# A list scheduler's durations of TensorE instructions replaced by others: the same 13,025 instructions in another order

## Chip, cores and metric

The kernel runs on one core of one Trainium2 chip. The metric is device time in microseconds (us) of one execution; the number compared is the median of several runs of the same program. Five engines run side by side, each with its own stream of instructions in a fixed order: TensorE (PE for its products, PEld for the loads of its weights), VectorE (DVE), ScalarE (ACT), GpSimd (POOL) and SyncE (SP, which issues the transfers).

## What is computed

Two blocks of two layers each on 256 tokens of 1024 features, in fp32, with a memory of 256 tokens. Cut to what matters:

```python
def first_block(x, mem, ...):
    for l in range(DEPTH):                                   # DEPTH = 2
        x = x + 0.5 * swiglu(rms_norm(x, ffn1_norm[l]), ffn1_w_in[l], ffn1_w_out[l])
        z = rms_norm(x, mix_norm[l]) @ w_mix_in[l]
        z_mla, z_swa, z_na = jnp.split(z, [MLA_IN, MLA_IN + SWA_IN], axis=-1)
        o = jnp.concatenate([rms_norm(mla_mixer(z_mla, ...), ...),   # latent attention, 8 heads
                             rms_norm(swa_mixer(z_swa, ...), ...),   # windowed, 4 heads
                             rms_norm(na_mixer(z_na, ...), ...)])    # neighbourhood, 4 heads
        x = x + o @ w_mix_out[l]
        x = x + mem_xattn(rms_norm(x, mem_norm_x[l]), mem, ...)
        x = x + 0.5 * swiglu(rms_norm(x, ffn2_norm[l]), ffn2_w_in[l], ffn2_w_out[l])
        x = rms_norm(x, block_norm[l])
```

The second block has, per layer, a mixer of two attentions (one of three branches with compressed keys, 8 heads, and one over blocks, "MoBA", 8 heads), gates of the branches, an output product and a third feed-forward, all modulated by columns worked out from a condition vector.

## The kernel before

**Products.** Every weight is an fp32 matrix that arrives in chunks of 128 x 1024 (`wr`, 512 KB). `wload` (line 455) splits a chunk into a high part `wh` (a cast, on ACT or DVE) and a low part `wl` (a subtraction, on DVE). The activations are split the same way into `xh` and `xl` (or two tiles `g`). `mm3` (line 481) then issues three fp32r products for each pair of operands (`wh`,`xh`; `wl`,`xh`; `wh`,`xl`), 128 x 512 at most, and `proj` (line 487) sums them over the k-tiles for both token tiles of 128. The 8570 instructions of TensorE are 6984 such fp32r products, 56 in bf16 (masks), and 1530 in plain fp32: transposes against an identity (`ps<-ident,g`) and the small products of the attentions.

**Between products.** The head norms and rotations of a projection (`heads` at line 1170, the latent part of `mixer` at line 759) are a chain: a product ends in PSUM; ACT squares it; DVE sums it per head; POOL raises the sums to the power -1/2 (`rstd`, line 429); DVE multiplies, rotates in four operations and adds; TensorE transposes the outcome. A softmax (`softmax_rows`, line 550) is a chain of the same kind: scores, DVE maximum, ACT exponential, DVE reciprocal, a scaling on ACT or DVE, four transposes.

**What sets the order.** The program is first traced in its natural order into a `Plan` as 13,025 instructions, each with its dependences. `Plan.schedule` (line 257) plays them through on paper: each engine has a time at which it is free, each instruction a duration from the table `Plan.cost` (line 231), and a result reaches TensorE from another engine `slack` = 400 ns after its end. At each step an engine takes, of the instructions that could start within 25 ns of the earliest (TensorE; other engines use a share of the duration), the one that stands first in the trace. So where TensorE would have to wait for a chain, a product of a later projection goes in between, and the transposes that the chain ends in go in as soon as the plan believes them ready:

```python
first = min(found, key=lambda f: f[:2])                       # line 328
lim = first[0] + (window if e == "tensor" else wait_for * cost(first[2], e))
s, pr, o = min((f for f in found if f[0] <= lim), key=lambda f: f[1])
...
e = min(o.ways, key=lambda w: max(free[w], at) + cost(o, w) + (spare if w == "vector" else 0))
```

The last line chooses ACT or DVE for an instruction that both can do. `emit` (line 385) then hands all instructions to their engines in that order, which is why every row of the profile bears line 385. On the chip nothing is reordered: an engine whose next instruction is not ready waits. The rest of the table, for the engines other than TensorE, is the same before and after the change (n: elements per partition):

```python
if eng == "gpsimd":
    return 300.0 + 165.0 * n if fn == "tensor_tensor" else 150.0
...
if eng == "scalar":
    return (51 if psum else 93) + n / 1.2 + 93 * cols
...
return 69 + n / (1.92 if fast else 0.96) + 62 * col          # DVE
```

Of the kernel before, what the change touches and what calls it, by code (L numbers as in the profile page):

```python
# [10 lines left out]
F32R = mybir.dt.float32r  # L11
BF = mybir.dt.bfloat16
# [6 lines left out]
# buffers: weight chunks (raw, split), transposed operands, activations of 1 and 2 KB a partition,  # L19
# columns, PSUM banks (and how many of them the attention may hold)  # L20
B = {"wr": 7, "wh": 7, "wl": 7, "xh": 4, "xl": 4, "g1": 11, "g2": 36, "sm": 40, "ps": 8, "psa": 6}
TAIL = (10, 12)      # k-tiles of a feed-forward's output halves in which one token tile goes ahead
# places in the trace by which some instructions give way to later ones
HP = (100, 3)        # products of the compression: the first, and each after it
XN = 300             # the block norm of the residual
XS = (43, 52, 60)    # parts of the input
# [10 lines left out]
CH = 1024          # columns of a weight chunk  # L37
# [21 lines left out]
# The kernel is traced in its natural order into a Plan. The Plan gives every  # L59
# instruction its place in the engines' streams by list scheduling (an engine takes  # L60
# the earliest instruction of the trace whose operands and buffers are there), and
# then hands them to Tile in that order. Tile places the buffers and the waits.

TABLE = {AF.Exp: 1, AF.Tanh: 1, AF.Silu: 2, AF.Sin: 3}     # which activations share a table


class VTile:
    def __init__(self, plan, pool, shape, dtype, tag, bufs, psum, share):
# [4 lines left out]
        self.acc = []                    # (op, p0, p1, mask, write, start)  # L73
        self.first = self.last = None    # trace positions
# [3 lines left out]
class View:  # L78
    """A slice of a tile: what it covers, and how to make it from the real one."""
# [81 lines left out]
class Plan:  # L161
# [6 lines left out]
    def tile(self, pool, shape, dtype, tag, bufs=1, psum=False, share=None):  # L168
        """share: (name, n): at most n of the tag's buffers may be held under that name"""
# [7 lines left out]
    @contextmanager  # L177
    def shift(self, by):
        """instructions traced inside rank as if they came `by` places later"""
        self.bias += by  # L180
        yield
        self.bias -= by

    # ---- tracing
    def either(self, *ways):
        """one instruction that several engines can carry out: (engine, fn, args, kw)"""
        return self.record(*ways[0], others=ways[1:])
# [1463 lines left out]
```

## Time and profile before

| | |
|---|---|
| median of 3 runs | 1945.27 us (1941.7 to 1947.16) |
| profiled execution: span from its first to its last instruction | 1940.7 us |
| profiled execution: time outside the span | not recorded |
| TensorE busy (products) | 1905.7 us, 98% of the span |
| DVE, ACT, POOL busy | 1438.1, 874.7, 119.9 us |
| read from HBM | 360.38 MB, 186 GB/s over the span |

How to read it: a product is in flight longer than it holds the engine, and the next one starts before it ends; a "busy" TensorE therefore also hides short gaps, and the distance from one start to the next tells the real pace. An instruction's idle time is put down to the engine whose result came last.

### The profile page before, as it was taken

To read this page: it belongs to the slowest core of one execution; us is meant where nothing else is said; L and a number is where in the kernel's file an instruction comes from. 1 tells how busy PE (TensorE), PEld (TensorE's weight loads), DVE (VectorE), ACT (ScalarE), POOL (GpSimd) and SP (SyncE) were. 2 spreads that over 40 slices of the span, in tenths; PEclk is the share of its full clock that TensorE was granted. 3 is DMA by queue.
4 is the path that set the end of the run, shared out by engine and by line. 5 is a ranking of instruction groups with operands and counts; after the bars stand their busy time and mean duration, and the time that the engine had idled before them with its cause. 6 is when DMAs were issued, how large, how long until landed. Compare 5 with 4: busy or idle time off the path is not lost.

```text
span 1940.7 us, 24909 instructions
## 1 busy us (share of the span) xinstructions
PE 1905.7 (98%) x9061; PEld 1512.4 (78%) x9062; DVE 1438.1 (74%) x2330; ACT 874.7 (45%) x1664; POOL 119.9 (6%) x98
## 2 busy tenths in 40 slices
PE   8999999999999999999999999999999999999999
PEld 6888867788887888767888766787888857787887
DVE  7875887898688866878986667578865867487664
ACT  5331675643243434657442455534431455435431
POOL 0000301100000001301000112000000102000000
PEclk9999999999999999999999999999999999999999
DMA  8776523388578856235885432357855513454561
GB/s 306 266 253 208 180 97 98 117 316 289 185 246 300 276 192 185 75 98 167 295 274 193 143 131 87 125 186 232 297 187 186 184 44 120 141 183 165 191 198 65
DMA packets 105242, 363.05 MB, mean 187 GB/s; under 512 B 13216, under 2 KB 15136, under 8 KB 105120
## 3 DMA queue, kind: packets, MB, share of 16 engines
q1 hardware_dynamic: 105120, 361.47, 55.5%
q8 instruction: 71, 1.16, 0.2%
q14 instruction: 51, 0.42, 0.1%
HBM read 360.38 MB, written 1.05 MB: 186 GB/s over the span
## 4 chain that ended last, share of the span: by engine, by line
PE 85%; DVE 7%; ACT 3%; POOL 3%; DMA 1%; issue 1%; SPq 0%; POOLq 0%; ACTq 0%; DVEq 0%
PE ps L385 85%; POOL sm L385 3%; DVE g L385 2%; ACT g L385 2%; DVE sm L385 2%; DVE wl L385 1%; DMA wr<-ffn_in_in 1%; DVE x L385 1%; DVE wh L385 0%; ACT wh L385 0%; ACT junk L385 0%; DMA inv<-inv_in 0%; DMA wr<-in_qa_in 0%; DMA x<-x_in 0%; ACT xh L385 0%
## 5 line engine op out<-in xcount | busy, mean ns | idle before, releaser
L385 DVE TENSOR_TENSOR wl<-wr,wh 128x1024 fp32r<-128x1024 f32 (+1 forms) x572 | 689.8, 1214 | 76.2 <-ACT wh L385 59.0
L385 PE MATMUL ps<-wh,xh 128*128 128x512 f32 (+3 forms) x1600 | 626.3, 392 | 3.6 <-ACT xh L385 1.3
L385 PE MATMUL ps<-wh,xl 128*128 128x512 f32 (+3 forms) x1600 | 623.4, 390 | 0.2 <-DVE xl L385 0.2
L385 PE MATMUL ps<-wl,xh 128*128 128x512 f32 (+3 forms) x1600 | 620.1, 388 | 0.0
L385 ACT CAST wh<-wr 128x1024 fp32r<-128x1024 f32 (+1 forms) x370 | 386.0, 1045 | 307.4 <-PE ps L385 279.8
L385 PE MATMUL ps<-wh,g 128*128 128x512 f32 (+1 forms) x1456 | 460.8, 393 | 0.2
L385 PEld LDWEIGHTS ps<-wh,xh 128*128 128x128 f32 x1600 | 302.2, 189 | 60.9 <-ACT xh L385 2.6
L385 PEld LDWEIGHTS ps<-wh,xl 128*128 128x128 f32 x1600 | 301.7, 189 | 58.6 <-DVE xl L385 1.8
L385 PEld LDWEIGHTS ps<-wl,xh 128*128 128x128 f32 x1600 | 302.1, 189 | 54.9 <-issue 1.5
L385 PEld LDWEIGHTS ps<-wh,g 128*128 128x128 f32 x1456 | 271.9, 188 | 57.4 <-issue 3.0
L385 PE MATMUL ps<-wl,g 128*128 128x512 f32 (+1 forms) x728 | 285.0, 392 | 0.0
L385 ACT ACTIVATE g<-ps,sm 128x256 f32<-128x256 f32 (+5 forms) x337 | 157.3, 488 | 169.4 <-PE ps L385 155.4
L385 POOL TENSOR_TENSOR sm<-sm,mhalf 128x1 f32<-128x1 f32 (+6 forms) x76 | 117.0, 1541 | 1474.8 <-DVE sm L385 1440.6
L385 DVE CAST wh<-wr 128x1024 fp32r<-128x1024 f32 (+2 forms) x202 | 139.0, 689 | 90.3 <-PE ps L385 89.4
L385 PE MATMUL ps<-ident,g 128*128 128x128 f32 (+1 forms) x942 | 157.3, 276 | 18.6 <-DVE g L385 10.7
L385 PEld LDWEIGHTS ps<-ident,g 128*128 128x128 f32 (+1 forms) x942 | 111.0, 141 | 78.8 <-ACT g L385 22.7
L385 PE MATMUL ps<-g,g 128*64 128x256 f32 (+8 forms) x728 | 171.8, 375 | 0.3
L385 DVE TENSOR_TENSOR g<-ps,g 128x256 f32<-128x256 f32 (+3 forms) x158 | 89.7, 568 | 109.2 <-ACT g L385 71.5
L385 PEld LDWEIGHTS ps<-wl,g 128*128 128x128 f32 x728 | 136.8, 188 | 28.4 <-issue 1.7
L385 PEld LDWEIGHTS ps<-g,g 128*64 128x64 f32 (+5 forms) x728 | 91.8, 161 | 52.1 <-issue 17.8
L385 ACT ACTIVATE junk<-x 128x512 bf16<-128x512 f32 x56 | 35.3, 630 | 189.1 <-DVE x L385 184.4
L385 ACT COPY g<-ps 128x512 f32<-128x512 f32 (+5 forms) x173 | 76.9, 467 | 93.2 <-PE ps L385 89.4
(93 smaller groups left out, 1008.1 us busy)
## 6 DMA issues: line engine op xcount, KB each, us to landing
wr<-ffn_in_in SPq DMA_DIRECT2D x264, 512.0 KB, 4.6
wr<-ffn_out_in SPq DMA_DIRECT2D x132, 512.0 KB, 4.2
wr<-ada_in SPq DMA_DIRECT2D x96, 512.0 KB, 4.7
wr<-in_gate_in SPq DMA_DIRECT2D x32, 512.0 KB, 3.5
wr<-in_b_in SPq DMA_DIRECT2D x24, 512.0 KB, 4.6
wr<-mix_out_in SPq DMA_DIRECT2D x16, 512.0 KB, 4.6
wr<-w_out_in SPq DMA_DIRECT2D x16, 512.0 KB, 4.6
wr<-mix_swa_in SPq DMA_DIRECT2D x8, 512.0 KB, 5.2
```

The lines of the kernel that those rows point to most:

```text
L385: getattr(getattr(self.nc, o.eng), fn)(*[r(a) for a in args], **{k: r(v) for k, v in kw.items()})
```

## The change

Two lines of `Plan.cost` give other durations (ns) for TensorE's products. Nothing else that is executed differs (the file also lost its comments, which have no effect).

```diff
@@ Plan.cost
         if eng == "tensor":
             if fn == "transpose":
                 return 109.0
             if ins[0].dtype == F32:
-                return max(n * 4 / 2.4, 213.0) * (0.52 if outs[0].shape[0] <= 64 else 1.0)
-            return max(n / 2.4, 107.0 if ins[0].dtype == F32R else 53.0) + 2.5
+                return 2 * max(n * 2 / 2.4 + 2, 109.0)
+            return max(n / 2.4 + 14, 109.0 if ins[0].dtype == F32R else 67.0)
```

An fp32r product of 512 columns goes from 215.8 to 227.3 ns, of 256 columns from 109.2 to 120.7; a plain fp32 product of 256 columns from 426.7 to 430.7, or from 221.9 to 430.7 where its output has at most 64 partitions (probabilities times values).

The order changes from the first mixer on; the feed-forwards keep theirs but for a few places. Of the casts and copies that ACT or DVE may do, five casts of weights (`wh<-wr`) go from ACT to DVE (365 and 207 of 572 instead of 370 and 202). Three places follow. `g2_88` and the like are tiles of activations, `ps` PSUM banks, the numbers behind names are those of buffers, and a row with x4 is four transposes.

TensorE, first block, first layer, latent attention: the transposes of the second token tile's normed queries and keys (`g2_88`, `g2_92`) among the products of the neighbourhood projection that fill the time of the chain. Before:

```order
L385 MATMUL ps_2249<-wh_2027,xl_1830 128x512
L385 MATMUL ps_2249<-wh_2027,xh_1822 128x512
L385 MATMUL ps_2249<-wl_2038,xh_1822 128x512
L385 MATMUL ps_2286<-ident_69,g2_88 128x128 x4
L385 MATMUL ps_2292<-ident_69,g2_92 128x128 x4
L385 MATMUL ps_2249<-wh_2067,xh_1822 128x512
```

And now:

```order
L385 MATMUL ps_2253<-wl_2027,xh_1562 128x512
L385 MATMUL ps_2253<-wh_2016,xl_1572 128x512
L385 MATMUL ps_2279<-ident_69,g2_88 128x128 x4
L385 MATMUL ps_2287<-ident_69,g2_92 128x128 x4
L385 MATMUL ps_2253<-wh_2029,xh_1821 128x512
L385 MATMUL ps_2253<-wl_2036,xh_1821 128x512
```

The eight transposes stand five 512-column products earlier, counted from the product that starts their chain.

TensorE, second block, first layer, MoBA: the transposes of the first token tile's keys (`g2_11154` before, `g2_11150` now) among the products of the next projection. Before:

```order
L385 MATMUL ps_11211<-wh_11107,xl_10117 128x512
L385 MATMUL ps_11211<-wh_11169,xh_10102 128x512
L385 MATMUL ps_11252<-ident_69,g2_11154 128x128 x4
L385 MATMUL ps_11211<-wl_11200,xh_10102 128x512
L385 MATMUL ps_11211<-wh_11169,xl_10117 128x512
```

And now:

```order
L385 MATMUL ps_11209<-wh_11063,xh_10092 128x512
L385 MATMUL ps_11209<-wl_11119,xh_10092 128x512
L385 MATMUL ps_11221<-ident_69,g2_11150 128x128 x4
L385 MATMUL ps_11209<-wh_11063,xl_10097 128x512
L385 MATMUL ps_11209<-wh_11074,xh_10092 128x512
```

Between the last product of these keys' own projection and the transposes stood 43 products of 512 columns, and 29 stand there now. For the second tile's keys it was 43 and is 33. The second layer has the same pattern.

DVE at the same place, the norm and rotation of these keys (`TENSOR_REDUCE` is the sum per head, `TENSOR_SCALAR` what POOL waits for, the rows from there on the rotation). Before:

```order
L385 TENSOR_REDUCE sm<-g_11162 128x8
L385 TENSOR_SCALAR sm<-sm 128x8
L385 TENSOR_TENSOR wl<-wr,wh 128x1024 x2
L385 TENSOR_TENSOR g_11154<-g_11154,sm 128x512
L385 TENSOR_TENSOR g_11234<-g_11154,g_9027 128x512
L385 TENSOR_TENSOR g_11239<-g_11154,g_9027 128x8x32 x2
L385 TENSOR_TENSOR g_11154<-g_11234,g_11239 128x512
```

And now:

```order
L385 TENSOR_REDUCE sm<-g_11155 128x8
L385 TENSOR_SCALAR sm<-sm 128x8
L385 TENSOR_TENSOR wl<-wr,wh 128x1024
L385 CAST wh<-wr 128x1024
L385 TENSOR_TENSOR g_11150<-g_11150,sm 128x512
L385 TENSOR_TENSOR g_11196<-g_11150,g_8822 128x512
L385 TENSOR_TENSOR g_11203<-g_11150,g_8822 128x8x32 x2
L385 TENSOR_TENSOR g_11150<-g_11196,g_11203 128x512
```

A cast has taken the place of one of the two subtractions; the chain itself has the same rows.

## Rows read from the trace of the kernel before

**Rows 1.** The page: busy us by engine (share of the span) and count.
```profile
PE 1905.7 (98%) x9061; PEld 1512.4 (78%) x9062; DVE 1438.1 (74%) x2330; ACT 874.7 (45%) x1664; POOL 119.9 (6%) x98
```

**Rows 2.** The page: the chain that ended last, by engine.
```profile
PE 85%; DVE 7%; ACT 3%; POOL 3%; DMA 1%; issue 1%; SPq 0%; POOLq 0%; ACTq 0%; DVEq 0%
```

**Rows 3.** Stretches: length, PE, PEld, DVE, ACT, POOL busy; clock, DMA share, GB/s.
```profile
200.00:300.00 100.00, 94.84 (x511) 73.83 (x510) 81.26 (x184) 70.56 (x179) 20.80 (x13) 1.00 0.40 129
...
1400.00:1500.00 100.00, 100.00 (x451) 82.43 (x450) 65.17 (x73) 29.55 (x40) 0.00 (x0) 1.00 0.60 196
```

**Rows 4.** Timeline of PE, 600 to 606 us: start, length (us), instruction.
```profile
600.57 0.40 PE L385 MATMUL ps<-wh,xh 128*128 128x512 f32 x1
...
605.82 0.39 PE L385 MATMUL ps<-wh,xl 128*128 128x512 f32 x1
```

**Rows 5.** Timeline of PE, 262 to 276 us: probabilities times values, two records each.
```profile
263.12 1.08 PE L385 MATMUL ps<-g,g 128*64 128x256 f32 x4
264.13 0.39 PE L385 MATMUL ps<-wh,xl 128*128 128x256 f32 x1
```

**Rows 6.** Groups by form: count | busy us, mean ns | idle before and releasers.
```profile
L385 DVE TENSOR_TENSOR wl<-wr,wh 128x1024 fp32r<-128x1024 f32 x554 | 672.4, 1222 | 67.6 <-ACT wh L385 50.5
...
L385 ACT CAST wh<-wr 128x1024 fp32r<-128x1024 f32 x357 | 375.0, 1052 | 265.9 <-PE ps L385 245.4 <-DMA wr<-ffn_in_in 9.9 <-DMA wr<-in_kv_in 3.4
...
L385 DVE CAST wh<-wr 128x1024 fp32r<-128x1024 f32 x197 | 136.1, 692 | 88.3 <-PE ps L385 87.4 <-DMA wr<-ffn_in_in 0.7
...
L385 POOL TENSOR_TENSOR sm<-sm,mhalf 128x8 f32<-128x8 f32 x16 | 38.0, 2378 | 167.3 <-DVE sm L385 154.1 <-ACT wh L385 11.5 <-ACT g L385 1.7
```

**Rows 7.** The chain of waits, 222 to 256 us: start, length, what.
```profile
237.14 5.28 POOL sm L385
```

**Rows 8.** Timeline of PE, 242 to 245 us; in brackets idle time and releaser.
```profile
241.80 0.39 PE L385 MATMUL ps<-wl,xh 128*128 128x512 f32 x1
244.07 1.17 PE L385 MATMUL ps<-ident,g 128*128 128x128 f32 x8 [1.88 <-DVE g L385]
```

**Rows 9.** Timeline of PE, second block, first layer: chain's last product, then its transposes.
```profile
1194.63 0.39 PE L385 MATMUL ps<-wh,xl 128*128 128x512 f32 x1
...
1204.88 0.39 PE L385 MATMUL ps<-wh,xh 128*128 128x512 f32 x1
1205.50 0.63 PE L385 MATMUL ps<-ident,g 128*128 128x128 f32 x4 [0.23 <-DVE g L385]
1205.89 0.48 PE L385 MATMUL ps<-wl,xh 128*128 128x512 f32 x1
```

**Rows 10.** Timeline of PE: the same transposes in the second layer.
```profile
1628.64 0.63 PE L385 MATMUL ps<-ident,g 128*128 128x128 f32 x4 [0.25 <-DVE g L385]
```

**Rows 11.** Timeline of DVE, 1198 to 1212 us.
```profile
1202.54 0.69 DVE L385 TENSOR_TENSOR g<-g,sm 128x512 f32<-128x512 f32 x1 [0.39 <-POOL sm L385]
```

**Rows 12.** A stretch of 10 us, second block, first layer (columns as in rows 3).
```profile
1200.00:1210.00 10.00, 9.77 (x46) 7.79 (x45) 9.09 (x13) 5.06 (x10) 4.94 (x2) 1.00 0.47 159
```

**Rows 13.** Timeline of PE: second layers of both blocks, two transposes at the end of chains.
```profile
795.85 0.63 PE L385 MATMUL ps<-ident,g 128*128 128x128 f32 x4 [0.73 <-DVE g L385]
...
1537.61 0.63 PE L385 MATMUL ps<-ident,g 128*128 128x128 f32 x4 [0.69 <-ACT wh L385]
```

**Rows 14.** Timeline of PE: waits in attention whose products are now longer covered.
```profile
362.25 0.50 PE L385 MATMUL ps<-wh,xh 128*128 128x512 f32 x1 [0.46 <-ACT g L385]
...
381.00 0.41 PE L385 MATMUL ps<-ident,g 128*128 128x128 f32 x2 [0.36 <-DVE g L385]
...
808.01 0.77 PE L385 MATMUL ps<-ident,g 128*128 128x128 f32 x5 [1.33 <-ACT g L385]
...
855.06 0.66 PE L385 MATMUL ps<-ident,g 128*128 128x128 f32 x4 [0.48 <-ACT g L385]
```

**Rows 15.** Stretches of 10 us with a lower granted clock (columns as in rows 3).
```profile
1110.00:1120.00 10.00, 10.00 (x62) 9.00 (x61) 8.07 (x11) 5.31 (x8) 0.52 (x1) 0.83 0.69 219
...
1590.00:1600.00 10.00, 10.00 (x32) 4.66 (x33) 3.15 (x11) 4.87 (x18) 0.00 (x0) 0.72 0.00 0
```

## The prediction

> **What bounds the kernel now.** I read the page first: products keep TensorE busy 98% of the span, DVE 74%, ACT 45% [rows 1]. The page's chain agrees: 85% of the way to the end is TensorE's own work, and the rest, some 15%, runs over DVE, ACT and POOL [rows 2]. The stretches of 100 us then show where that rest lies: 100.00 of 100 us busy in a feed-forward (1400 to 1500 us), 94.84 in the first mixer (200 to 300 us), where DVE and ACT are also fullest [rows 3]. The change issues the same instructions, so it can only win or lose the gaps of the mixers, and the order shows that the feed-forwards hardly move.
>
> Busy time hides short gaps, so the pace has to come from starts: from 600.57 to 605.82 us there are 24 products of 512 columns, 23 steps, 0.228 us each [rows 4]. That is the new table's 227.3 ns, not the old 215.8. Probabilities times values, 64 partitions out, take (264.13 - 263.12)/2 = 0.505 us each [rows 5]: the old table said 0.222, the new one says 0.431. So the new figures are nearer the chip. But a plan lives by the ratio of TensorE's time to that of the chains it covers, and the other engines keep figures that are too short: DVE's subtraction of 1024 elements is planned at 1.14 us and takes 1.222, its cast 0.60 against 0.692, ACT's cast 0.95 against 1.052, POOL's power of 8 columns 1.62 against 2.378 [rows 6]. Before, everything was planned too fast by similar shares; now only the chains are.
>
> **The first latent chain.** At 237.14 us POOL begins the power of 16 columns, planned at 300 + 16 x 165 ns = 2.94 us; it takes 5.28, and DVE's rotation follows [rows 7]. TensorE's last product before the transposes starts at 241.80, they start at 244.07: the step is 2.27 instead of 0.228 us, so some 2.0 us are lost, of which 1.88 shows as idle on DVE [rows 8]. There was no spare cover, and the new order takes five products away: 5 x 0.228 = **+1.1 us**, if the chain is no quicker.
>
> **MoBA's keys, twice.** From the keys' last product (1194.63) to their transposes (1205.50) pass 10.9 us, and the transposes already wait: 1204.88 to 1205.50 is 0.62 instead of 0.23 us [rows 9]. Of 43 covering products 29 remain: 14 x 0.228 = 3.2 us. The second tile's keys lose ten products, 2.3 us, but their chain runs while TensorE waits for the first, so I count the larger alone. Could the chain shorten instead? DVE is busy 9.09 of 10 us there [rows 12], and the order keeps its rows. One subtraction gives way to a cast, 1.222 to 0.692 us [rows 6], but both stand between DVE's hand-over to POOL and POOL's answer, where DVE waits 0.39 us for POOL in any case [rows 11]. So nothing is gained. The second layer shows the same wait, at 1628.64 us [rows 10], and the same cuts: 2 x 3.2 = **+6.4 us**. If the second tile's cut came on top, 2 x 2.3 = 4.6 more.
>
> **Second layers.** The transposes at 795.85 us waited 0.73 us [rows 13]. Their cover loses 29 products of 512 columns and 3 of half that length (30.5 x 0.228 = 7.0 us) and gains 8 score products, 6 transposes and 2 masks: 8 x 0.505 [rows 5], 6 x 0.1 (four take 1205.89 - 1205.50 = 0.39 us) [rows 9], 2 x 0.228 = 5.1 us. The scores' and masks' prices are borrowed from the rows that they are nearest to. **+1.9 us**. The transposes at 1537.61 waited 0.69 [rows 13]; they lose one product and some small ones: between 0.2 and 1.4 us, taken **+0.8**.
>
> **What is gained.** Four waits get more cover than they miss: 0.46, 0.36, 1.33 and 0.48 us [rows 14], together **-2.6**. In the first mixer's attention up to eight products that stood ahead of transposes now stand behind them; ACT's stream there is shortened too, by work moved behind, so this is between 0 and 8 x 0.228 = 1.8 us a layer, taken as 0 because TensorE was ready late there, not early. The five casts that go to DVE run beside products, on an engine that is free a quarter of the time [rows 1], and are put at nothing; with that cover gone they would cost 5 x 0.692 us [rows 6]. No transfer moves in a way that matters: DMA's share of the chain is 1% [rows 2].
>
> **Sum.** 1.1 + 6.4 + 1.9 + 0.8 - 2.6 = +7.6 us on a span of 1940.7. The median of the runs is 1945.27, 4.6 above that span; on it the sum gives **1953 us**. Products taken out of a cover are not lost: they come later, where TensorE was not waiting, so they win nothing back. That is the step that I trust least.
>
> **A rule against the change.** The starts say 0.228 us a product [rows 4]. The Trainium skill, page "TensorE: Matmul & The Clock Gate", section "Back-to-back issue gap", gives columns/2.4 + 2.5 ns for an isolated product at full clock, which is 215.8 ns at 512 columns, to the digit the old table; by it the new table would be the wrong one. The trace contradicts it here by 12 ns. With 0.216 the terms made of products would shrink by 5%, and the sum would be 7.1 instead of 7.6 us.
>
> **Rivals.** *Nothing measurable* (28%): the waits inside the chains shorten by as much as the covers. For it: of the 10.9 us [rows 9] only some 7 are the chain's own instructions (a square, a sum, POOL's 2.4, five DVE steps), the rest is queueing behind other work, which a new order could lift. Against it: DVE full [rows 12] and the same rows in its order. Time: 1945 plus or minus 3. The same few waits would then stand at other places.
>
> *Faster* (23%): one mechanism, at the ends of the attentions. A plan that knows that a product of probabilities and values costs 0.431 and not 0.222 us spends fewer projections on each head, and has them left where it ran out. Price: the four waits that vanish, 2.6 us, and the falls of the clock that follow thin stretches. The granted clock averages 0.83 from 1110 to 1120 us and 0.72 from 1590 to 1600 [rows 15], so a part of each stretch ran at the lower of its two levels, 1.2 instead of 2.4 GHz. In the second, TensorE starts only 32 products in 10 us. The two stretches lose 0.17 x 10 + 0.28 x 10 = 4.5 us. If both falls went and no chain became longer than its cover: -2.6 - 4.5 = -7.1, that is 1938 us. It decides if the waits of rows 9 and 10 stay at 0.6 us or less. Against it: the covers before the long chains shrink in the order, visibly.
>
> *Worse than forecast* (inside the 49% for slower): the second tile's cuts add (4.6), both layers of the first mixer's attention lose 1.8 (3.6), and longer waits bring one more fall of the clock in each layer of the second block (4.5 for the two): 7.6 + 12.7 = 20.3, that is 1966 us.
>
> **How the numbers follow.** Forecast and its worse form 49%, no difference 28%, faster 23%. A measurement of this kernel can tell about 0.3%, 5.8 us, from no change (its three runs lie within 5.5). Slower by more than that, over 1951.1, is the first case; the second is the middle. The range runs from the full price of the faster rival to the full price of the worse form, each with one us for the scatter of the runs, 1937 to 1967 us; the forecast's own range, from 4 to 15 us of added waiting, is 1949 to 1960.
>
> **What would show it.** In the new profile the pace in feed-forwards stays 0.228 us. The waits that end in transposes grow: about 3.1 us at the first latent chain's `ps<-ident,g` x8 (2.0 before), 3.6 us at the keys' transposes near 1205 and 1630 us (0.4 and 0.4 before), while those near 808 and 855 us shrink. TensorE's idle time behind DVE and ACT, summed in the list of waits, rises by some 8 us, and the stretch from 1200 to 1210 us shows PE near 7 of 10 instead of 9.77 [rows 12]. I would be wrong if the transposes of the keys start without a wait, which would mean that the chains have sped up with the new order; or if the sum of waits grows while the time does not, which would mean that the products moved behind fill gaps that I took for none.

## The result, and the profile after

| | before | after |
|---|---|---|
| median (4 runs each, side by side) | 1944.79 us (1941.7 to 1947.16) | 1966.2 us (1964.28 to 1972.17) |
| ratio | 1 | 1.0111, 95% interval 1.009 to 1.0132 |
| span of the profiled execution | 1940.7 us | 1963.9 us |

The change costs 21 us. The forecast was 1953 us, a loss of 8; the time lies inside its range of 1937 to 1967 us, at the upper edge.

The page after, busy time and the chain that ended last. They answer to [rows 1, 2].

```profile
PE 1909.2 (97%) x9060; PEld 1514.3 (77%) x9062; DVE 1435.2 (73%) x2331; ACT 869.1 (44%) x1662; POOL 113.9 (6%) x98
...
PE 73%; DVE 11%; DMA 5%; ACT 4%; issue 3%; POOL 3%; POOLq 0%; SPq 0%; DVEq 0%; ACTq 0%
PE ps L385 73%; DMA wr<-ada_in 4%; DVE wl L385 4%; DVE g L385 3%; POOL sm L385 3%; ACT g L385 2%; DVE sm L385 1%; DVE wr L385 1%; DVE wh L385 1%; ACT wh L385 1%; DMA wr<-ffn_in_in 1%; ACT junk L385 0%; DVE x L385 0%; ACT xh L385 0%; DVE xl 
```

The busy shares moved by one point, which tells nothing. The chain tells more: TensorE's own share fell from 85 to 73%, and transfers rose from 1 to 5%, nearly all of it `wr<-ada_in`, 4%. These are the 96 chunks of the condition vector's matrix ("ada" below). `ada_steps` (line 1062) loads a chunk of 512 KB, and one DVE step, `SCALAR_TENSOR_TENSOR wr<-wr,c`, multiplies it with the vector and sums it. These steps have nothing to do with the products beside them; they are traced between the parts of a feed-forward to fill DVE's free time.

The list of waits says who waits for them. First after (columns: engine, what, who released it, us in total, times, the longest):

```profile
DVE wr L385 <- DMA wr<-ada_in: 30.8, 16, 3.8
PE ps L385 <- DVE g L385: 28.3, 35, 2.6
...
PE ps L385 <- ACT g L385: 9.3, 12, 1.9
```

and the same three before:

```profile
PE ps L385 <- DVE g L385: 11.4, 19, 1.9
...
PE ps L385 <- ACT g L385: 6.8, 12, 1.3
...
DVE wr L385 <- DMA wr<-ada_in: 5.0, 2, 2.5
```

TensorE waits 19.4 us more for DVE and ACT, and DVE 25.8 us more for one kind of transfer.

**Where the time goes** is seen when the two traces are laid side by side by work: wherever both orders have issued the same set of TensorE instructions, the start of the next one is compared. The changed kernel is 0.3 us behind at 49 us of the span, 8.9 behind at 124, 8.4 at 341, 11.0 at the end of block 1 (1089), 14.9 after the first layer of block 2 (1324), 22.4 after the second (1700) and 23.2 at the end. So 8.6 us are lost in the first feed-forward, little in the rest of block 1, some 12 in block 2. TensorE's added waits for DVE and ACT lie at the same places: up to 130 us they sum to 8.7 us after and 1.1 before, from there to 1095 us to 16.2 and 14.8, and behind it to 17.3 and 6.8.

The first feed-forward in stretches of 10 us, after (columns as in rows 3):

```profile
60.00:70.00 10.00, 8.96 (x42) 7.15 (x41) 6.55 (x11) 2.48 (x4) 0.00 (x0) 1.00 0.77 263
70.00:80.00 10.00, 9.03 (x43) 7.14 (x42) 7.52 (x10) 4.18 (x6) 0.00 (x0) 1.00 0.82 263
```

Before, the first of them read:

```profile
60.00:70.00 10.00, 10.00 (x46) 8.20 (x45) 6.98 (x10) 3.41 (x5) 0.00 (x0) 1.00 0.72 238
```

The clock is full (1.00), but TensorE starts 42 products where it started 46. DVE's timeline after, from the split that feeds the next products on, shows why:

```profile
64.31 0.69 DVE L385 TENSOR_TENSOR g<-ps,g 128x512 fp32r<-128x512 f32 x1
68.43 1.23 DVE L385 SCALAR_TENSOR_TENSOR wr<-wr,c 128x1024 f32<-128x1024 f32 x1 [3.43 <-DMA wr<-ada_in]
69.58 0.08 DVE L385 DVE_READ_ACCUMULATOR wr<-wr,c 128x1 f32 x1
69.58 0.48 DVE L385 SCALAR_TENSOR_TENSOR g<-ps,sm,g 128x256 f32<-128x256 f32 x1
```

and the same place before:

```profile
61.73 0.69 DVE L385 TENSOR_TENSOR g<-ps,g 128x512 fp32r<-128x512 f32 x1 [0.24 <-ACT g L385]
62.34 1.22 DVE L385 SCALAR_TENSOR_TENSOR wr<-wr,c 128x1024 f32<-128x1024 f32 x1
63.48 0.08 DVE L385 DVE_READ_ACCUMULATOR wr<-wr,c 128x1 f32 x1
65.31 0.48 DVE L385 SCALAR_TENSOR_TENSOR g<-ps,sm,g 128x256 f32<-128x256 f32 x1 [1.75 <-ACT g L385]
```

The last row of each is the gating product of the feed-forward, `g<-ps,sm,g`, which the next transposes need. Before, the ada step ran at once and the gating product waited for ACT, its proper source. After, the ada step stands in the same gap, but its chunk is not there: DVE sits 3.43 us, and the gating product, in line behind it, starts 5.3 us after the split instead of 3.6 (64.31 to 69.58; before 61.73 to 65.31). The transfer behind that wait was issued at 62.79 us; the view of `ada_in`, the matrix in memory, says how long the transfers issued from 55 to 80 us took to land:

```profile
DMA to landing us min/median/max: 5.2/5.4/5.5
```

So the chunk lands at some 68.2 us. The plan had allowed 4.5 us from issue to step (1.46 for the transfer, 2.0 for its landing, the rest in turn behind others). TensorE pays at the end of that line; seven such waits stand between 50 and 127 us, and before there was none. One of them, in TensorE's timeline after:

```profile
63.21 0.44 PE L385 MATMUL ps<-ident,g 128*128 128x128 f32 x2 [1.04 <-DVE g L385]
```

**The places that the forecast named**, after, in order of time: the first latent chain, two places in the second layer of block 1, the keys of MoBA in the first layer of block 2 (the product that starts the first tile's chain, then both tiles' transposes), a chain that the forecast had not listed, and the keys in the second layer.

```profile
252.67 1.62 PE L385 MATMUL ps<-ident,g 128*128 128x128 f32 x8 [2.59 <-DVE g L385]
...
804.55 0.63 PE L385 MATMUL ps<-ident,g 128*128 128x128 f32 x4 [1.08 <-DVE g L385]
...
833.49 0.66 PE L385 MATMUL ps<-ident,g 128*128 128x128 f32 x4 [0.66 <-ACT g L385]
...
1206.36 0.39 PE L385 MATMUL ps<-wh,xl 128*128 128x512 f32 x1
...
1215.54 0.63 PE L385 MATMUL ps<-ident,g 128*128 128x128 f32 x4 [1.07 <-DVE g L385]
1223.28 0.63 PE L385 MATMUL ps<-ident,g 128*128 128x128 f32 x4 [0.75 <-DVE g L385]
...
1536.01 1.59 PE L385 MATMUL ps<-ident,g 128*128 128x128 f32 x8 [1.95 <-ACT g L385]
...
1646.77 0.63 PE L385 MATMUL ps<-ident,g 128*128 128x128 f32 x4 [1.09 <-DVE g L385]
1654.51 0.63 PE L385 MATMUL ps<-ident,g 128*128 128x128 f32 x4 [0.71 <-DVE g L385]
```

The latent chain's idle time rose from 1.88 [rows 8] to 2.59 us. The transposes at 804.55 us are, by the order, those that stood at 795.85 before [rows 13]: 0.73 us became 1.08. Those at 833.49 started without a wait before. The waits at 808 and 855 us [rows 14] are gone, and so is the one at 1537.61 [rows 13]. The keys wait 1.07 and 0.75 us in the first layer and much the same in the second.

The keys lost the cover that the forecast counted, 14 products of 43, and yet they wait only 0.84 us longer than before (1.07 against 0.23 [rows 9]), because their chain became shorter. From its product to the transposes pass 9.2 us now (1206.36 to 1215.54) and passed 10.9 before. DVE's timeline shows where: the sum per head, before and after,

```profile
1199.00 0.68 DVE L385 TENSOR_REDUCE sm<-g 128x8 f32<-128x512 f32 x1
```

```profile
1209.04 0.68 DVE L385 TENSOR_REDUCE sm<-g 128x8 f32<-128x512 f32 x1
```

starts 4.4 us after the chain's product before (1194.63 to 1199.00), with another tile's rotation and two casts of weights in line ahead of it on DVE, and 2.7 us after it now (1206.36 to 1209.04), with the rotation alone ahead of it.

**The clock.** A stretch at a granted clock under 1 is counted here as its length times what is missing; read in steps of 4 us, that is 8.0 us of the span before and 13.4 after.

### The profile page after: what moved, and what is told of

Read it like the earlier page. It is cut to its first block, busy times and chain, and to the rows that moved or that the text cites. A ratio compares the mean times of both kernels' runs of the same rounds, so it can differ in the third digit from the quotient of the medians.

```text
span 1963.9 us, 24946 instructions
## 1 busy us (share of the span) xinstructions
PE 1909.2 (97%) x9060; PEld 1514.3 (77%) x9062; DVE 1435.2 (73%) x2331; ACT 869.1 (44%) x1662; POOL 113.9 (6%) x98
## 4 chain that ended last, share of the span: by engine, by line
PE 73%; DVE 11%; DMA 5%; ACT 4%; issue 3%; POOL 3%; POOLq 0%; SPq 0%; DVEq 0%; ACTq 0%
PE ps L385 73%; DMA wr<-ada_in 4%; DVE wl L385 4%; DVE g L385 3%; POOL sm L385 3%; ACT g L385 2%; DVE sm L385 1%; DVE wr L385 1%; DVE wh L385 1%; ACT wh L385 1%; DMA wr<-ffn_in_in 1%; ACT junk L385 0%; DVE x L385 0%; ACT xh L385 0%; DVE xl L385 0%
## 5 line engine op out<-in xcount | busy, mean ns | idle before, releaser
L385 DVE TENSOR_TENSOR wl<-wr,wh 128x1024 fp32r<-128x1024 f32 (+1 forms) x572 | 687.5, 1214 | 58.4 <-ACT wh L385 46.2
L385 PE MATMUL ps<-wh,xh 128*128 128x512 f32 (+3 forms) x1600 | 628.5, 393 | 2.9 <-ACT xh L385 1.6
L385 PE MATMUL ps<-wh,xl 128*128 128x512 f32 (+3 forms) x1600 | 624.3, 390 | 0.1
L385 PE MATMUL ps<-wl,xh 128*128 128x512 f32 (+3 forms) x1600 | 623.2, 390 | 0.6 <-DVE wl L385 0.6
L385 ACT CAST wh<-wr 128x1024 fp32r<-128x1024 f32 (+3 forms) x365 | 380.6, 1045 | 322.4 <-PE ps L385 297.3
L385 PE MATMUL ps<-wh,g 128*128 128x512 f32 (+1 forms) x1456 | 460.6, 393 | 0.0
L385 PEld LDWEIGHTS ps<-wh,xh 128*128 128x128 f32 x1600 | 303.4, 190 | 58.7 <-ACT xh L385 3.2
L385 PEld LDWEIGHTS ps<-wl,xh 128*128 128x128 f32 x1600 | 303.4, 190 | 57.5 <-issue 2.6
L385 PEld LDWEIGHTS ps<-wh,xl 128*128 128x128 f32 x1600 | 302.7, 189 | 58.1 <-issue 1.9
L385 PEld LDWEIGHTS ps<-wh,g 128*128 128x128 f32 x1456 | 272.0, 188 | 57.3 <-issue 3.8
L385 PE MATMUL ps<-wl,g 128*128 128x512 f32 (+1 forms) x728 | 284.9, 392 | 0.0
L385 ACT ACTIVATE g<-ps,sm 128x256 f32<-128x256 f32 (+4 forms) x340 | 158.7, 487 | 185.5 <-PE ps L385 159.8
L385 DVE CAST wh<-wr 128x1024 fp32r<-128x1024 f32 (+1 forms) x207 | 142.3, 689 | 94.4 <-PE ps L385 93.3
L385 POOL TENSOR_TENSOR sm<-sm,mhalf 128x1 f32<-128x1 f32 (+6 forms) x76 | 110.9, 1469 | 1494.5 <-DVE sm L385 1374.0
L385 PE MATMUL ps<-ident,g 128*128 128x128 f32 (+1 forms) x942 | 157.7, 278 | 36.2 <-DVE g L385 25.4
L385 PEld LDWEIGHTS ps<-ident,g 128*128 128x128 f32 (+1 forms) x942 | 108.3, 141 | 103.3 <-DVE g L385 24.5
L385 PE MATMUL ps<-g,g 128*64 128x256 f32 (+8 forms) x728 | 166.5, 373 | 0.6 <-DVE g L385 0.3
L385 DVE TENSOR_TENSOR g<-ps,g 128x256 f32<-128x256 f32 (+3 forms) x158 | 89.7, 567 | 100.0 <-ACT g L385 62.5
L385 PEld LDWEIGHTS ps<-wl,g 128*128 128x128 f32 x728 | 136.9, 188 | 26.9 <-issue 0.8
L385 DVE SCALAR_TENSOR_TENSOR wr<-wr,c 128x1024 f32<-128x1024 f32 x96 | 116.2, 1219 | 30.9 <-DMA wr<-ada_in 30.8
L385 PEld LDWEIGHTS ps<-g,g 128*64 128x64 f32 (+4 forms) x728 | 90.9, 160 | 50.1 <-issue 14.8
L385 ACT ACTIVATE junk<-x 128x512 bf16<-128x512 f32 x56 | 35.3, 630 | 183.5 <-DVE x L385 178.7
```

What stands on the lines that cost most here:

```text
L385: getattr(getattr(self.nc, o.eng), fn)(*[r(a) for a in args], **{k: r(v) for k, v in kw.items()})
```

## The experiments

"Delay" is the distance to the kernel before by the same work, as above. The runs are called e1 to e15. All edits concern the plan alone; the instructions stay the same. Where a row bears another line than L385, it is `emit` moved down by the edit. Each was timed in five rounds beside the kernel before, whose median was 1943.3 to 1945.2 us.

### Which line of the change

```diff
-                return 2 * max(n * 2 / 2.4 + 2, 109.0)
+                return max(n * 4 / 2.4, 213.0) * (0.52 if outs[0].shape[0] <= 64 else 1.0)
```

> Edit: only the fp32r line of the change (512 columns 215.8 to 227.3 ns); plain fp32 products keep the old figures. Theory A (the new fp32r pace puts a step of the condition vector on DVE ahead of a gating product in the first feed-forward, before its transfer has landed, about 5.3 us after its issue; this costs 8.6 us there; the feed-forwards have no plain fp32 products other than transposes): the first feed-forward shows the same seven waits of 1 to 1.5 us before its transposes, +8 to +9 us by 120 us of the span, and the whole is 1955 to 1966 us, depending on what the attentions do. Theory B (the longer figure for probabilities times values, 0.222 to 0.431 us, thins the covers of all chains, and is the larger part of the loss): without it the time is 1945 to 1952 us, and the loss shows in the other half of the change.

Measured (e1): 1974.82 us, ratio 1.014 (1.0109 to 1.0172). Delay 7.8 us at 124, 14.4 at the end of block 1, 29.3 at the end.

```diff
-            return max(n / 2.4 + 14, 109.0 if ins[0].dtype == F32R else 67.0)
+            return max(n / 2.4, 107.0 if ins[0].dtype == F32R else 53.0) + 2.5
```

> Edit: only the plain fp32 line of the change (probabilities times values 221.9 to 430.7 ns); fp32r products keep the old figures. Theory A: the feed-forwards keep the order of before, so no waits before the transposes of the first feed-forward (nothing of the 8.6 us); the whole is 1943 to 1952 us. Theory B (the figure for probabilities times values does most of the harm in the attentions): slower by most of the 21 us, 1957 to 1966 us, all of it in mixers and block 2.

Measured (e2): 1945.42 us, ratio 1.0001 (0.9985 to 1.0017). Delay -0.7 us at 124, -9.3 at the end of block 1, +3.2 at the end.

So the loss as a whole comes with the 11.5 ns more for an fp32r product, and theory B falls. The doubled figure for probabilities times values is not harmless, though: e2 is 9.3 us ahead at the end of block 1 and gives 12.5 back in block 2, 8.5 of them in one stretch at half clock (1636 to 1656 us). Both are taken up below. Whether this line takes something off beside the other one (1974.82 against 1966.2) is not shown: of e1's six executions two took some 1963 us at a mean granted clock of 0.994, and four 1972 to 1980 us at 0.985 to 0.989.

### The first feed-forward

The cleanest test puts the new fp32r figure into the plan for the instructions of the first feed-forward alone (`Plan.new` is set at the start of the first call of `ffn` and cleared at its end):

```diff
+            return max(n / 2.4 + 14, 109.0 if ins[0].dtype == F32R else 67.0) if Plan.new else \
+                max(n / 2.4, 107.0 if ins[0].dtype == F32R else 53.0) + 2.5
```

> Edit: the kernel before, with the new fp32r figure for the instructions of the first feed-forward alone (the plan's old figures everywhere else). TensorE's order then differs from before in 13 rows of 8570, DVE's steps of the condition vector in the first feed-forward stand 4.5 to 6 us behind their issue as in the changed kernel, and the attentions keep the order of before. Theory A (these steps wait on DVE for transfers that land later than planned): seven waits of 1 to 1.5 us before transposes by 127 us, +8 to +9 us in all, 1953 to 1955 us. Theory B (the loss needs the thinner covers of the attentions too): within 3 us of before.

Measured (e9): 1953.53 us, ratio 1.0051 (1.0035 to 1.0068). The delay is 8.6 us at 124 and 8.0 to 8.6 from there to 1109 us; 13 rows of TensorE are enough. DVE waits for the same transfers:

```profile
DVE wr L387 <- DMA wr<-ada_in: 23.0, 7, 3.8
```

The other way round, the changed kernel with the true landing time for these transfers alone:

```diff
-                end = dma + 2000
+                end = dma + (3800 if ... == "ada_in" else 2000)
```

> Edit: the changed kernel, with the planned time from the end of a transfer's turn to its use raised from 2000 to 3800 ns for the transfers of the condition vector's matrix alone (plan only; nothing is left out). The order of the attentions of block 1 is then that of the changed kernel, while the steps in the feed-forwards are planned 6 to 10 us after their issue instead of 4.5 to 6. Theory A (transfers that land later than planned): the seven waits of the first feed-forward go, DVE's idle time behind these transfers falls from 30.8 us to under 8, and the time falls by 8 to 10 us to 1956 to 1958. Theory B (chains too short of cover everywhere, the transfers only named because they came last): the waits move to another releaser and the time stays within 3 us of 1966.

Measured (e3): 1960.88 us, ratio 1.0077 (1.0056 to 1.0098), against 1.0111 for the change. The stretch of the first feed-forward is whole again, 46 products:

```profile
60.00:70.00 10.00, 10.00 (x46) 8.25 (x45) 7.79 (x12) 3.51 (x6) 0.00 (x0) 1.00 0.78 272
```

DVE's wait for `ada_in` is no longer in the list, and by 127 us this run is 8.2 us ahead of the changed kernel, with the same products in the same order but for 155 rows. That the median shows 5 of these 8 has a likely reason in the clock: in the profiled execution 6.8 us went at half clock at 884 to 904 us, with the order of the changed kernel (see the last section), and five of this run's six executions had a mean granted clock of 0.989 to 0.991, the four of the changed kernel 0.992 to 0.995. Theory A's mechanism holds, shown in both directions; its time of 1956 to 1958 us was missed by 3.

### Block 1 and block 2 apart

The change in block 1 alone; `Plan.b2` is set where block 2 is traced. Here the fp32r line, and the fp32 line likewise:

```diff
+            if Plan.b2:
+                return max(n / 2.4, 107.0 if ins[0].dtype == F32R else 53.0) + 2.5
             return max(n / 2.4 + 14, 109.0 if ins[0].dtype == F32R else 67.0)
```

> Edit: the change in block 1 alone; block 2 is planned with the old figures. At the end of block 1 the changed kernel is 11 us behind the kernel before, and block 2 adds 12. If the two parts add (theory H): 1953 to 1957 us, with the seven waits of the first feed-forward and no new ones after 1100 us. If block 2 loses because of the state in which block 1 leaves the queues and buffers (theory I): 1962 to 1968 us, as with the whole change.

Measured (e13): 1952.17 us, ratio 1.0043 (1.0028 to 1.0059). Delay 7.9 us at 124, 7.7 at the end of block 1, 6.5 at the end.

And in block 2 alone, with the test turned round:

```diff
-            if Plan.b2:
+            if not Plan.b2:
```

> Edit: the change in block 2 alone; block 1 is planned with the old figures. The change in block 1 alone took 1952 us, 8.9 more than the kernel before. If the blocks add (theory H), this one has the other 12 to 13 us: 1954 to 1959 us, lost after 1100 us at waits before transposes near 1205, 1330, 1630 and 1760 us and in stretches at half clock. If the losses need each other (theory I): under 1950 us.

Measured (e15): 1955.77 us, ratio 1.0061 (1.0049 to 1.0073). Delay 0.1 us at 1093, 7.3 at 1324, 13.6 at 1700. Together 0.0043 + 0.0061 = 0.0104, against 0.0111 for the whole: the blocks add, and block 1's share is its first feed-forward. Theory H.

### What block 2 loses

First the term on which the forecast laid most: the keys' cover. On top of the corrected ada transfers, only the keys' transposes are planned later:

```diff
-                    lat = slack if "tensor" in x.ways else 200.0 if e == "tensor" else 130.0
+                    lat = slack + x.late if "tensor" in x.ways else 200.0 if e == "tensor" else 130.0
```

> Edit: the changed kernel with the condition vector's transfers planned 1800 ns later (1961 us so far), and the transposes of MoBA's keys alone planned 3200 ns later, so that the 14 products taken from their cover stand there again; 152 rows of TensorE move, 76 in each layer of block 2. Theory F (the forecast's term: the cut covers of the keys cost up to 3.2 us a layer; the waits seen there are 2.3 us a layer): the waits before these transposes fall under 0.3 us and the time falls by 4 to 6 us, to 1955 to 1957 us. Theory G (the loss of block 2 comes from other chains and from falls of the clock, and products held back here are missed elsewhere): the waits go and the time falls by less than 2 us.

Measured (e11): 1962.68 us, ratio 1.0099 (1.0077 to 1.0122), against 1960.88 for e3, on which it is built, so no gain. The waits did go; the same transposes now read

```profile
1215.10 0.60 PE L386 MATMUL ps<-ident,g 128*128 128x128 f32 x4
1221.71 0.60 PE L386 MATMUL ps<-ident,g 128*128 128x128 f32 x4
```

without a bracket, and around them this run gains 1.9 us in the first layer and 2.6 in the second on e3. But 6.8 us go at half clock right behind, at 1228 to 1244 us, and that was no single case: all four executions had a mean granted clock of 0.983 to 0.987, the six of e3 0.989 to 0.993, which is an estimated 8 us more at half clock (28.4 against 20.6, the medians of what is missing from 1 times the span). A term that was real in its place was no gain in the whole: theory G.

Then the other side of the ratio: in block 2 DVE, ACT and POOL also get measured figures.

```diff
-            return 300.0 + 165.0 * n if fn == "tensor_tensor" else 150.0
+            return np.interp(n, (1, 2, 4, 6, 8, 16), (925, 1196, 1349, 1485, 2378, 4221)) if fn == "tensor_tensor" else 205.0
-            return (51 if psum else 93) + n / 1.2 + 93 * cols
+            return (160 if psum else 200) + n / 1.2 + 97 * cols + 93 * ("accum_out" in kw)
-        return 69 + n / (1.92 if fast else 0.96) + 62 * col
+        return 155 + n / (1.92 if fast else 0.96) + 62 * col + 82 * ("accum_out" in kw)
```

> Edit: the changed kernel with the condition vector's transfers planned 1800 ns later (1961 us so far), and for block 2 alone the figures of DVE, ACT and POOL also set to measured ones; transfers as before. Theory J (block 2 loses because only TensorE's figures were corrected, so that chains are planned too fast against the products that cover them): block 2 loses nothing against the kernel before, 1947 to 1951 us, and TensorE's idle time in block 2 falls from 17 us to under 9. Theory K (block 2 loses by transfers that land late, and the run that moved every figure gained there for that reason): 1957 to 1963 us.

Measured (e14): 1944.42 us, ratio 1.0001 (0.999 to 1.0012); 1960.88 without the three lines. Over block 2 the delay goes from +3.8 us (1089) to -0.2 at the end. TensorE's waits from 1095 us to the end, in e3, which lacks the three lines:

```profile
PE ps L385 <- ACT g L385: 6.8, 7, 2.0
PE ps L385 <- DVE g L385: 6.7, 8, 1.2
PE ps L385 <- ACT wh L385: 2.1, 3, 1.1
PE ps L385 <- ACT xh L385: 1.1, 3, 0.5
```

and in this run:

```profile
PE ps L390 <- DVE g L390: 2.7, 4, 1.1
PE ps L390 <- DVE xh L390: 2.4, 2, 2.2
PE ps L390 <- ACT xh L390: 2.1, 1, 2.1
PE ps L390 <- ACT g L390: 1.8, 4, 0.8
```

Theory J, and the time came out even better than it said. Block 2 loses 12 us because one side of a ratio was corrected: with the other side corrected too the loss is gone, though the transfers of the weights are planned as before. It is spread over many chains: 16.7 us of waits at 21 places become 9.0 at 11. Which of the three lines does most is not shown.

### All figures, and better versions

The three lines of e14 for the whole kernel (there they stood behind `Plan.b2`), transfers as they were:

> Edit: the changed kernel, with the planned durations of DVE, ACT and POOL also set to what the rows show (DVE's constant 69 to 155 ns, ACT's 51 and 93 to 160 and 200, the sum over a row 82 to 93 more, POOL's powers 925 to 4221 ns by columns). Theory A: two things change, the steps in the first feed-forward stand 10 to 12 us behind their issue, which takes 8 us away, and the chains of the attentions get longer covers; 1945 to 1957 us. Theory B (the table is only consistent when all engines are set, and the covers of MoBA's keys, the first latent chain and the second layers were cut because the chains' figures stayed too short): the waits of 1 to 2.7 us before transposes near 253, 1215 and 1647 us shrink below 0.6 us and the time is at or under that of before, 1935 to 1945 us. If neither holds, the time stays near 1966 us.

Measured (e5): 1949.36 us, ratio 1.0021 (1.001 to 1.0033). Theory A's number: the first feed-forward is whole (delay -0.1 at 121 us), block 2 gains 2.8 us, and 10.2 us are lost in block 1's attentions, 8.5 of them in two stretches at half clock (264 to 276 and 892 to 900 us). With every transfer landing 1800 ns later as well:

```diff
-                end = dma + 2000
+                end = dma + 3800
```

> Edit: the plan's figures of all engines set to measured ones and every transfer planned to land 1800 ns later (3800 instead of 2000 ns after its turn). The run with all engines' figures but the old transfers took 1949 us. Theory A (transfers that land later than planned are worth something wherever a step stands close behind its transfer; that run's first feed-forward had none left): no gain in the first feed-forward, 0 to 4 us elsewhere, 1944 to 1950 us. Theory C (what is left is falls of the clock, 16.7 us at the lower level against 8.0 before): within 3 us of 1949 us.

Measured (e6): 1939.82 us, ratio 0.9981 (0.9969 to 0.9993). Neither theory said a time so low. The measured table, once it is complete, is as good as the one that was too fast throughout, by a hair better. 9.9 us of this run were lost to the lower clock, against 16.7.

A coarser cure, on top of e3: a product that waits for another engine is planned 1 us later.

```diff
-    def schedule(self, window=200.0, wait_for=0.2, slack=400.0, spare=0.0, ahead=1500.0):
+    def schedule(self, window=200.0, wait_for=0.2, slack=1400.0, spare=0.0, ahead=1500.0):
```

> Edit: the kernel with the condition vector's transfers planned 1800 ns later, and in addition the plan's gap between the end of a chain on another engine and the product that uses it raised from 400 to 1400 ns. Theory B (in the attentions the covers before the chains' transposes are about 1 us too thin, because DVE, ACT and POOL keep figures that are too short): the waits of 0.6 to 2.7 us before transposes near 253, 1215 and 1647 us shrink below 0.8 us each, TensorE's idle time behind DVE falls by half, and the time falls from 1961 to 1945 to 1953 us. Theory C (what is left over is falls of the clock, 19.9 us at the lower level in that run against 8.0 before, and these come from single waits that a deeper plan does not remove): the time stays between 1955 and 1965 us, with as many stretches at a granted clock of 0.5.

Measured (e7): 1941.8 us, ratio 0.9991 (0.9978 to 1.0005). Theory B, and better than it said; the keys wait 0.62 to 0.65 us, only the first latent chain stays above 0.8, at 1.04. The profiled execution was 10.7 us ahead at 821 us and ended 6.1 behind, with 25.0 us lost to the lower clock; at 1948.61 us it is 6.8 above the median.

The fp32 line in block 1 alone; block 2, and fp32r products everywhere, keep the old figures:

```diff
+                return 2 * max(n * 2 / 2.4 + 2, 109.0) if Plan.new else \
+                    max(n * 4 / 2.4, 213.0) * (0.52 if outs[0].shape[0] <= 64 else 1.0)
```

> Edit: the plain fp32 line of the change alone, in block 1 only; block 2 and all fp32r products are planned with the old figures. The run with that line everywhere was 9.3 us ahead of the kernel before at the end of block 1 and lost 12 us in block 2, 8.5 of them by a stretch at half clock at 1636 to 1656 us. Theory D (the right figure for probabilities times values helps the attentions of block 1 and the loss of block 2 comes with block 2's own order): 1934 to 1940 us, ahead of both kernels. Theory E (the gain of block 1 and the loss of block 2 are scatter from one profiled run to the next): 1942 to 1948 us, as before.

Measured (e8): 1936.36 us, ratio 0.9961 (0.9949 to 0.9973); delay -7.3 us at the end of block 1 and -7.0 at the end. Theory D: the -9.3 us of the fp32 line were no scatter. What they consist of was not settled: TensorE's waits in that run sum to about as much as before. Against e2, which has the same line in block 2 as well (1.0001, 0.9985 to 1.0017), the intervals do not meet: in block 2 this line costs some 8 us (1945.42 against 1936.36, each beside its own before), without any fp32r figure having moved.

Two mixtures by `Plan.b2`: block 2 as in e6, block 1 as in e7, and then block 1 as in e8.

```diff
+                end = dma + (3800 if o.b2 or ... == "ada_in" else 2000)
+                    lat = (400.0 if x.b2 else slack) if "tensor" in x.ways else 200.0 if e == "tensor" else 130.0
```

> Edit: block 1 planned with the change, the condition vector's transfers 1800 ns later and the gap before products 1400 instead of 400 ns; block 2 with measured figures for all engines, transfers planned 1800 ns later and the gap at 400 ns. The run with the first part had 10.7 us less than before at 821 us and 6.3 at the end of block 1, after a stretch of 5.1 us lost at half clock; the run with the second part gained 3.7 us over block 2. Theory H (blocks independent): 1932 to 1938 us. Theory I: 1938 to 1944 us, with falls of the clock as in the first run (25 us lost at the lower level).

Measured (e10): 1937.5 us, ratio 0.997 (0.9957 to 0.9984); 11.4 us ahead at 821, 5.4 at the end, 15.0 us lost to the lower clock. That lies half a microsecond inside theory H and does not tell the two apart.

```diff
+                end = dma + (3800 if o.b2 else 2000)
+            return max(n / 2.4 + 14, 109.0 if ins[0].dtype == F32R else 67.0) if Plan.b2 else \
+                max(n / 2.4, 107.0 if ins[0].dtype == F32R else 53.0) + 2.5
```

> Edit: block 1 planned with the plain fp32 line of the change alone, block 2 with measured figures for all engines and transfers planned to land 1800 ns later. The runs with one of the two had 7.3 us less than before at the end of block 1, and 3.7 us less over block 2. If the blocks are independent (theory H): 1932 to 1937 us, ahead of both kernels. If block 2's gain depended on its own block 1, or was scatter (theory I): 1936 to 1942 us.

Measured (e12): **1929.43 us, ratio 0.9931 (0.991 to 0.9951)**, the best of all and better than expected; delay -7.4 us at the end of block 1, -12.0 at 1700 us. It keeps block 1's old fp32r figure, so it is a find of this study and no rule.

## Why the prediction was right and where it failed

**Right: the sign, and its mechanism for block 2.** "Before, everything was planned too fast by similar shares; now only the chains are." Run e14 shows the second half: with the chains' figures set as well, block 2's loss is gone. "Similar shares" says too much: by the prediction's own figures the products were planned 5% too short, DVE's and ACT's instructions 7 to 13%, POOL's power 32% and probabilities times values 56%. The forecast had the direction from these durations [rows 5, 6]. A rule of the Trainium skill would have put it more generally: page "VectorE: DVE Perf Modes", section "The TRN2 errata", gives (columns + 151)/0.96 ns for an fp32 tensor-tensor; at 1024 columns that makes an estimated 1224 ns. The rows agree, 1222 ns [rows 6], where the plan had 1136.

**Wrong: "the feed-forwards hardly move", and "no transfer moves in a way that matters: DMA's share of the chain is 1%".** This is the step that failed, and it left out 8 to 10 us. TensorE's order in the first feed-forward does move in 13 rows only, but DVE's moves too, and TensorE's products wait for DVE. The prediction read the order of DVE at the keys and not here, because TensorE was 100% busy in a feed-forward [rows 3], as though an engine that never waits could not begin to. Here it did: the products hang on DVE's being punctual, and DVE's gaps are filled with steps whose transfers are planned to land too soon. Before, most of its steps stood 9.6 us or more behind their issue in the plan, and the plan's error did not show. A share of 1% says that nothing is late now; it says nothing of how near it is to being late. For that the distance from issue to use has to be read, and the time to landing beside it, 5.4 us.

On that time the Trainium skill, page "DMA: Bandwidth & Descriptors", section "Anatomy of one DMA — SWDGE (gpsimd) path", says some 2.0 us fixed and bytes/436e9 beside it, fitted on another path than the one used here; by it 512 KB would take an estimated 3.2 us. The measurement decides: 5.2 to 5.5 us, with the DMA engines 77 to 82% busy in those stretches.

**Wrong in size: block 2.** The forecast had 6.4 + 0.8 us. Run e15 measured 12 (0.0061 of 1943.6). The keys were not its core: the first tile's waited 0.84 us a layer more, where 3.2 was forecast, and PE from 1200 to 1210 us stood at 9.52 of 10, from 1210 to 1220 at 8.93, and not near 7. Here the step that failed is "So nothing is gained": the chain did shorten, by 1.7 us, since DVE took up the sum per head that much sooner. The rival that gave no difference had named this, queueing that a new order could lift. "I count the larger alone" was wrong as well: the second tile waited 0.5 to 0.6 us more. Their cover brought nothing back in the median (e11). The rest came at chains that had not been listed, as the 1.95 us at 1536.01 where there had been no wait, and at the lower clock.

**Wrong in size: the covers of the second layers and what is gained.** The term of +1.9 us at 795.85 came to 0.35, and the wait at 1537.61, taken at +0.8, went away. Of the four waits of [rows 14] three went as said and one stayed (0.36 us at 381, 0.35 at 389 now), but others grew beside them (from 0.32 to 0.93 us at 355, from nothing to 0.66 at 833). All the waits that the sum names, with both tiles of the keys, changed by +0.9 us together, where +7.6 was forecast; TensorE's waits for DVE and ACT as a whole rose by 19.4 us, where 8 was forecast. Block 1 without its first feed-forward came out near nothing (e9 and e13, without and with the rest of block 1, differ by 0.0008, 1.6 us, less than their intervals), so gains and losses cancel there, as the forecast's terms for it nearly do (+1.1, +1.9, -2.6).

**Right by luck: the "worse form" at 1966 us** gave the time, and with it the range holds it. Of its three additions only the falls of the clock stand, 5.4 us more than before in the profiled executions (13.4 against 8.0); the second tiles added some 1.1 us and not 4.6, block 1's attentions lost next to nothing, and the first feed-forward stands in the place of the rest. The faster rival's ground, that the figure for probabilities times values helps the ends of the attentions, holds for block 1 (e8: -0.4%) but not in the changed kernel, where the fp32r line is there too and block 2 is planned with it.

**The products' pace.** The new table's 227 ns is the true one: six steps from 600.46 to 601.84 us after the change take 0.230 us each. The measured figure alone made the kernel slower; with all other figures measured too it does not (e6).

## What to carry to other kernels

Correcting the figures of one engine in a planner's table moves every ratio between its work and the chains beneath it; that cost 1.1% here, while the full set of measured figures, landing times included, cost nothing. A complete table does not give the best order, though: a larger margin before the products did as well (e7), and two mixed tables were faster (e8, e12). Where the order changes on an engine that is 100% busy, look at the order of the engines that feed it: list what stands in line ahead of their next result, and for each such step compare the distance from its transfer's issue to its use with the landing time in the trace. And a wait that goes away in its place is no gain until the median says so.

## What the runs showed that was not expected

Stretches at half clock can differ between executions of one order. Runs e3 and e11 have the same order of TensorE and DVE up to 1100 us. The one read (columns as in rows 3)

```profile
884.00:888.00 4.00, 1.64 (x11) 1.00 (x10) 3.24 (x9) 3.62 (x12) 0.09 (x1) 0.91 0.42 131
888.00:892.00 4.00, 4.00 (x15) 2.59 (x15) 2.00 (x4) 2.52 (x6) 1.01 (x1) 0.50 0.79 204
892.00:896.00 4.00, 4.00 (x14) 2.83 (x13) 1.20 (x3) 0.75 (x3) 0.00 (x0) 0.50 0.22 77
```

and the other

```profile
888.00:892.00 4.00, 2.16 (x13) 1.33 (x14) 3.40 (x8) 4.00 (x14) 0.00 (x0) 1.00 0.40 108
892.00:896.00 4.00, 4.00 (x23) 2.71 (x23) 2.33 (x6) 2.46 (x8) 1.01 (x1) 1.00 0.76 256
```

Both have a thin stretch: TensorE was busy for 1.64 of 4 us at 884 to 888 in the first, for 2.16 at 888 to 892 in the second, which was 3.0 us behind by the same work. Then the first ran at 1.2 instead of 2.4 GHz, and the second did not; from 892 to 896 us they started 14 and 23 products, and by 901 us the second was 2.9 us ahead. Such falls were worth 1.7 to 10.2 us apiece, so two single profiles of this kernel can differ by as much as a whole term of the forecast, and only medians over several runs tell such terms apart. Even a median carries them where an order brings them in most executions, as in e11 and e1.
